# Interleaving the high and the low half of each weight block word by word

## The chip, the cores and the metric

The kernel runs on one core of a Trainium2 chip. The metric is the device time of one execution in microseconds, as the median of several runs. The profile is that of one execution.

## The reference

One step of a decoder layer for 256 prompt rows and 8 sample rows, 264 in all, with shared weights, all in float32:

```
h += 0.5 * swiglu(rmsnorm(h), gate, up, down)      # ffn1: 2048 -> 5504 -> 2048
u  = rmsnorm(h);  z = u @ w_in                     # pooling | RWKV-7 | attention queries | 3 gates
h += (g0 * pool(z) + g1 * rwkv7(z) + g2 * cross_attention(z, memory)) @ w_o
h += 0.5 * swiglu(rmsnorm(h), gate, up, down)      # ffn2
y  = rmsnorm(h)
mem_k, mem_v = rmsnorm(mem) @ w_mem_k, rmsnorm(mem) @ w_mem_v   # 256 memory tokens, 2048 -> 512
```

Outputs are y for both groups, the memory keys and values, and the recurrent states. Nearly all the arithmetic is products of a (264 x 2048) or (264 x 5504) activation with a weight matrix that is read once.

## The kernel before, in words

Activations are kept transposed: a tile holds 128 channels on the partitions and the 264 rows as columns. Each float32 product is made from three matmuls in the type fp32r, which carries fewer bits: every operand is split into a high half (its value rounded to fp32r) and a low half (the rest). The function `mm3` adds hi·hi, hi·lo and lo·hi into one accumulator. In it the weight is the stationary operand, a 128x128 tile that TensorE loads, and the activation is the moving operand, 264 columns.

The weights come as a stream of 783 blocks listed in `specs`, in the order of use. A block is usually eight tiles of 128x128, 1024 words on each partition (512 KB); 747 blocks have that size, 32 have 384 words, 2 have 512 and 2 have 256. `emit_load(i)` issues the transfer of block i on SP's queue into a `raw` buffer (5 of them), has ACT copy it to `whi` in the type fp32r, which rounds, and has DVE subtract `whi` from `raw` into `wlo` (3 buffers of each). `nxt` is called at the use of block i and first emits the loads up to block i + 2, so that a block is split while two earlier ones are multiplied. `proj` runs over the blocks of one output tile and calls `mm3` for each 128x128 tile.

One stage uses the weights differently: `mem_proj` projects the memory tokens. There the split tokens (`m0h`, `m0l`, ...) are the stationary operand, and the weight block is the moving one, 512 columns at a time (L517 to L519; 16 blocks, 192 matmuls).

The stages follow each other: the first feed-forward with the memory projections in its early part, the mixer's input projections with cross-attention and element-wise RWKV work beside them, the gates with the RWKV recurrence in the background (`tri_gen`, `chain_gen`, `sample_gen`, on DVE, POOL and TensorE), the output projections, the second feed-forward, and the last norm. Background work is written as generators, of which `tick` runs the due ones after each block. The instructions of an engine run in the order in which they were issued; the waits between engines are derived from which tiles an instruction reads and writes.

Two lines that the prediction also speaks of are in `tri_gen`, on tiles `c4k` with 32x32 matrices; the second source of the product is a column of the matrix, so its words lie 32 words apart:

```
DVE.tensor_tensor(out=tmp[:, 0:t, 0:t], in0=W[:, 0:t, 0:t],                                   # L977
                  in1=U[:, 0:t, t].unsqueeze(1).broadcast_to([P, t, t]), op=ALU.mult)
DVE.tensor_reduce(out=W[:, 0:t, t], in_=tmp[:, 0:t, 0:t], axis=AX.X, op=ALU.add)              # L979
```

and one is in the attention of the sample rows, where a 128x128 float32 tile is loaded for a moving operand of one column (L788).

Of the kernel before, what the change touches and what calls it, by code (L numbers as in the profile page):

```python
# [9 lines left out]
F32 = mybir.dt.float32  # L10
F32R = mybir.dt.float32r
AF = mybir.ActivationFunctionType
ALU = mybir.AluOpType
AX = mybir.AxisListType

P = 128
# [22 lines left out]
HK = 1024  # L39
# [7 lines left out]
def step_kernel(ctx: ExitStack, tc: tile.TileContext, I, O):  # L47
    nc = tc.nc
    PE, ACT, DVE, POOL, SP = nc.tensor, nc.scalar, nc.vector, nc.gpsimd, nc.sync
    PSUM = bass.MemoryType.PSUM  # L50
    DRAM = bass.MemoryType.DRAM
# [3 lines left out]
    wp = ctx.enter_context(tc.tile_pool(name="wp", bufs=3))  # L55
# [11 lines left out]
    def sb(pool, shape, tag, dt=F32, bufs=None):  # L67
        kw = {} if bufs is None else {"bufs": bufs}
        return pool.tile(shape, dt, tag=tag, name=nm(tag), **kw)

    def ps(shape=(P, 512)):
        return pms.tile(list(shape), F32, tag="ps", name=nm("ps"))
# [4 lines left out]
    def pool_ctx(name, side=None):  # L77
        kw = {} if side is None else {"side": side}
        cm = tc.tile_pool(name=name, bufs=1, reuse_waits="tile", **kw)
        return cm  # L80

# [1 line left out]
    ident = sb(cst, [P, P], "ident")  # L83
    make_identity(nc, ident)
    ones = sb(cst, [P, P], "ones")
# [21 lines left out]
    for t in range(15):  # L107
        DVE.memset(rcnt[:, t:t + 1], 1.0 / (t + 1))

# [1 line left out]
    def flat(a):  # L111
        return a[0]

# [54 lines left out]
    loaded = {}  # L168
# [3 lines left out]
    def emit_load(i):  # L172
        name, w, k0, n, c0, m = specs[i]
        raw = wp.tile([P, HK], F32, tag="raw", name=f"raw{i}", bufs=5)
        rv = raw[:, :n * m].rearrange("p (j c) -> p j c", c=m)
        ws = w if isinstance(w, tuple) else (w,)
        cw = m // len(ws)
        for q, wq in enumerate(ws):
            SP.dma_start(out=rv[:, :, q * cw:(q + 1) * cw],
                         in_=wq[k0 * P:(k0 + n) * P, c0:c0 + cw].rearrange("(j p) c -> p j c", p=P))  # L180
        hi = wp.tile([P, HK], F32R, tag="whi", name=f"whi{i}")
        ACT.activation(hi[:, :n * m], raw[:, :n * m], AF.Copy)  # L182
        lo = wp.tile([P, HK], F32R, tag="wlo", name=f"wlo{i}")
        DVE.tensor_tensor(out=lo[:, :n * m], in0=raw[:, :n * m], in1=hi[:, :n * m].bitcast(F32), op=ALU.subtract)  # L184
        loaded[i] = (hi[:, :n * m].rearrange("p (j c) -> p j c", c=m),
                     lo[:, :n * m].rearrange("p (j c) -> p j c", c=m))

    def spawn(gen, wait=0):
        tasks.append([state["t"] + wait + (not state["in"]), gen])
# [26 lines left out]
    def nxt(name):  # L216
        i = state["i"]
        assert specs[i][0] == name, (specs[i][0], name)
        while state["l"] <= min(i + state["look"], len(specs) - 1):
            emit_load(state["l"])  # L220
            state["l"] += 1
        state["i"] = i + 1
        loaded.pop(i - 3, None)
        tick()
        return loaded[i][0], loaded[i][1], specs[i][3]
# [14 lines left out]
                k += 1  # L240
        return acc

# [1 line left out]
    nstate = {}  # L244

    def norm_begin():
# [51 lines left out]
        later(wait, fin, nstate["sq"])  # L298
        return nstate["xs"], rstd

# [1 line left out]
    def dt_(name, shape):  # L302
        return dr.tile(list(shape), F32, tag=name, name=name)

# [11 lines left out]
    ys_d = dt_("ys_d", [NB, RW])  # L316
    qs_d = dt_("qs_d", [NB, XW])

# [1 line left out]
    hcm = pool_ctx("h1")  # L320
    hp = hcm.__enter__()
    fcm = pool_ctx("f1a")
# [17 lines left out]
    p = ps()  # L340
# [120 lines left out]
            x_squares(c)  # L461
        return accs

# [1 line left out]
    sst = sb(cst, [P, 27, NB], "sst")  # L465
    mx = []

# [69 lines left out]
            DVE.tensor_copy(out=ktt[:, hh:hh + 2, :], in_=p.rearrange("p (q m) -> p q m", q=2))  # L537
        SP.dma_start(out=KT_d, in_=ktt)

# [1 line left out]
    def ffn(pre, h, xs, rstd, done, pool, tpool, first=None, hook=None):  # L541
        gs = [None] * NF

        def glu(f, ag, au):
            t1 = sb(tpool, [P, NT], "t1", bufs=2)
            DVE.tensor_tensor(out=t1, in0=ag[:, :NT], in1=rstd, op=ALU.mult)
            s1 = sb(tpool, [P, NT], "s1", bufs=2)
            ACT.activation(s1, t1, AF.Sigmoid)  # L548
            POOL.tensor_tensor(out=t1, in0=t1, in1=rstd, op=ALU.mult)  # L549
            POOL.tensor_tensor(out=s1, in0=s1, in1=t1, op=ALU.mult)  # L550
            g = sb(tpool, [P, NT], "g", bufs=2)
            DVE.tensor_tensor(out=g, in0=au[:, :NT], in1=s1, op=ALU.mult)  # L552
            gs[f] = split(pool(f), g, f"g{f}")

        for f in range(NF):
            if hook is not None:
                hook(f)
            if f == 0 and first is not None:
                later(3, glu, 0, *first)
                continue  # L560
            ag = proj((pre, "g", f), KD, xs)
            au = proj((pre, "u", f), KD, xs)
            glu(f, ag, au)
        for d in range(KD):
            ad = proj((pre, "d", d), NF, gs)
            DVE.scalar_tensor_tensor(out=h[d], in0=ad[:, :NT], scalar=0.5, in1=h[d], op0=ALU.mult, op1=ALU.add)
            done(d)
# [30 lines left out]
    fcm.__exit__(None, None, None)  # L598
    hcm.__exit__(None, None, None)

# [1 line left out]
    mxcm = pool_ctx("mx")  # L602
    mp = mxcm.__enter__()
    Mcm = pool_ctx("M", side="right")
# [9 lines left out]
    s1cm = pool_ctx("sub1")  # L614
    ew = s1cm.__enter__()

# [1 line left out]
    spr = sb(ew, [120, PW], "BKt")  # L618
    SP.dma_start(out=spr, in_=I["state_pool"][0].rearrange("b r c -> (b r) c"))
    spT = sb(ew, [P, 4, 120], "spT")  # L620
# [17 lines left out]
    for g in range(4):  # L638
# [10 lines left out]
        while sh < w:  # L649
# [3 lines left out]
                               op=ALU.add)  # L653
# [22 lines left out]

    later(4, pool_rows)

# [1 line left out]
    for g in range(4):  # L680
        acc = proj(("zq", g), KD, xs)
        DVE.tensor_tensor(out=qT[g], in0=acc[:, :NT], in1=rstd, op=ALU.mult)
# [113 lines left out]
    spawn(attn_prompt(), 2)  # L796
    spawn(attn_sample(), 2)

# [1 line left out]
    def zmix(acc, m, idx, tag, out=None):  # L800
        z = sb(ew, [P, 15 + NT], "zt", bufs=2)
        POOL.memset(z[:m, 0:1], 0.0)
        DVE.tensor_tensor(out=z[:m, 1:1 + NT], in0=acc[:m, :NT], in1=rstd[:m], op=ALU.mult)
        POOL.tensor_copy(out=zlast[:m, idx, :], in_=z[:m, SEQ:SEQ + 9])
        df = sb(ew, [P, 15 + NT], "diff", bufs=2)
        POOL.tensor_tensor(out=df[:m, 0:SEQ], in0=z[:m, 0:SEQ], in1=z[:m, 1:1 + SEQ], op=ALU.subtract)
        POOL.tensor_tensor(out=df[:m, SEQ:NT], in0=sst[:m, idx, :], in1=z[:m, 1 + SEQ:1 + NT], op=ALU.subtract)
        x = sb(ew, [P, NT], tag) if out is None else out
        DVE.scalar_tensor_tensor(out=x[:m], in0=df[:m, 0:NT], scalar=col("rwkv_mu", idx)[:m],
                                 in1=z[:m, 1:1 + NT], op0=ALU.mult, op1=ALU.add)  # L810
        return x
# [128 lines left out]
        recv_mix(v, ft, acc)  # L940
        later(2, build_m, v, ft)

# [1 line left out]
    rp, s2cm, yT = None, None, None  # L944

    def c4(dt=F32):
# [270 lines left out]
    for dp in range(8):  # L1217
        ms = []
        for b, w, src in ((0, "pool_out", pl), (2, "xattn_out", list(zip(oh, ol)))):
            gt = [gate(b, d) for d in (2 * dp, 2 * dp + 1)]  # L1220
            wh, wl, n = nxt(w)
# [51 lines left out]
    xs, rstd = norm_end()  # L1273
    mhcm.__exit__(None, None, None)

# [1 line left out]
    fcm = pool_ctx("f2")  # L1277
    fp = fcm.__enter__()
    Y = []
# [34 lines left out]
    p = ps()  # L1314
    for i in range(3):
        for q, t in enumerate((sq, sql)):
            PE.matmul(p[:, 2 * i:2 * i + 2], lhsT=sqr[q] if i == 2 else t[:, i * P:(i + 1) * P], rhs=ones[:, 0:2],
                      start=q == 0, stop=q == 1)
# [64 lines left out]
```

## Time and profile before

| | |
|---|---|
| runs, us | 2464.16, 2472.68, 2472.36 (median 2472.36) |
| profiled execution | span 2464.4 us, from first to last instruction; no time of its own beside it is given |
| mean granted TensorE clock | 0.987 of full speed |
| PE matmul busy | 2419.3 us, 19702 matmuls |
| weight loads busy | 2377.5 us, beside the matmuls |
| DVE / ACT / POOL busy | 1452.2 / 1086.5 / 514.6 us |
| memory read | 430.19 MB, 182 GB/s over the span |

Busy times of different engines overlap. [...]

### The profile page before, as it was taken

The page shows a single profiled execution, that of the slowest core. Times are in us where ns is not written, and L with a number is a line of the kernel's source. Part 1 is how long each engine was busy: PE and PEld are TensorE (multiplying, and loading weights), DVE is VectorE, ACT ScalarE, POOL GpSimd, SP SyncE. Part 2 cuts the span into 40 slices and gives each one's busy share as a digit, 9 for nine tenths or more (in the row PEclk, how much of TensorE's full clock was granted, in tenths as well). Part 3 has the DMA queues.
Part 4 walks back from the last instruction along what each step waited for, and adds up shares of the span by engine and source line. Part 5 has one row for each costly group of instructions (what it writes and reads, how often), then busy time and mean ns, then how long its engine had stood idle before and what let it go on. Part 6 is the DMA issues. An engine that isn't in the chain of part 4 may idle for free.

```text
span 2464.4 us, 47553 instructions
## 1 busy us (share of the span) xinstructions
PE 2419.3 (98%) x19702; PEld 2377.5 (96%) x19702; DVE 1452.2 (59%) x1818; ACT 1086.5 (44%) x1436; POOL 514.6 (21%) x593
## 2 busy tenths in 40 slices
PE   8999999999999999999979999999999999999998
PEld 7999999999999988999979999999999999999998
DVE  6655555555444659798894765666555555544444
ACT  6444444444444445454322754444444444444444
POOL 3211211120000225461480210111111211110000
PEclk9999999999999999999889999999999999999999
DMA  8676666666666867676755667776666666666664
GB/s 231 172 216 180 180 179 180 180 180 177 186 189 192 243 181 215 170 185 184 189 157 150 159 181 192 195 220 178 179 180 180 180 180 181 180 173 175 176 182 129
DMA packets 822460, 452.03 MB, mean 183 GB/s; under 512 B 29092, under 2 KB 806982, under 8 KB 821963
## 3 DMA queue, kind: packets, MB, share of 16 engines
q1 hardware_dynamic: 821795, 448.91, 65.2%
q8 instruction: 154, 2.52, 0.4%
q14 instruction: 63, 0.52, 0.1%
q0 software_dynamic: 448, 0.08, 0.0%
HBM read 430.19 MB, written 18.96 MB: 182 GB/s over the span
## 4 chain that ended last, share of the span: by engine, by line
PE 93%; DVE 2%; DMA 2%; issue 1%; POOL 1%; ACT 0%; SPq 0%; DVEq 0%; POOLq 0%; ACTq 0%
PE acc L228 29%; PE acc L230 29%; PE acc L229 28%; DVE wlo L184 1%; DMA qb<-qs_d 1%; POOL kc L746 1%; PE acc L519 1%; PE acc L518 1%; PE acc L517 1%; PE ps L902 1%; PE acc L788 1%; PE ps L1080 0%; PE ps L1056 0%; PE ps L1084 0%; DMA raw<-in_ffn_w_up_dram 0%
## 5 line engine op out<-in xcount | busy, mean ns | idle before, releaser
L184 DVE TENSOR_TENSOR wlo<-raw,whi 128x1024 fp32r<-128x1024 f32 (+2 forms) x783 | 966.1, 1234 | 732.7 <-ACT whi L182 677.2
L182 ACT ACTIVATE whi<-raw 128x1024 fp32r<-128x1024 f32 (+2 forms) x783 | 809.9, 1035 | 1136.3 <-PE acc L229 757.2
L549 POOL TENSOR_TENSOR t<-t,rstd 128x264 f32<-128x264 f32 x86 | 123.0, 1430 | 855.8 <-ACT s L548 843.7
L272 POOL TENSOR_TENSOR sqs<-sqs,sqt 128x264 f32<-128x264 f32 x44 | 41.9, 953 | 547.4 <-ACT sqt L271 547.4
L230 PE MATMUL acc<-x8h,wlo 128*128 128x264 f32 (+1 forms) x255 | 72.9, 286 | 6.8 <-DVE wlo L184 6.8
L230 PE MATMUL acc<-x0h,wlo 128*128 128x264 f32 (+1 forms) x255 | 73.5, 289 | 5.0 <-DVE snm L690 3.6
L228 PE MATMUL acc<-x0h,whi 128*128 128x264 f32 (+1 forms) x255 | 77.8, 305 | 0.0
L228 PE MATMUL acc<-x8h,whi 128*128 128x264 f32 (+1 forms) x255 | 76.8, 302 | 0.0
L228 PE MATMUL acc<-x4h,whi 128*128 128x264 f32 (+1 forms) x255 | 73.5, 289 | 1.3 <-ACT x4h L261 1.3
L552 DVE TENSOR_TENSOR g<-acc,s 128x264 f32<-128x264 f32 x86 | 37.2, 432 | 63.4 <-PE acc L230 61.2
L230 PE MATMUL acc<-x1h,wlo 128*128 128x264 f32 (+1 forms) x255 | 73.9, 290 | 0.0
L229 PE MATMUL acc<-x1l,whi 128*128 128x264 f32 (+1 forms) x255 | 73.8, 290 | 0.0
L230 PE MATMUL acc<-x13h,wlo 128*128 128x264 f32 (+1 forms) x255 | 73.8, 289 | 0.0
L230 PE MATMUL acc<-x2h,wlo 128*128 128x264 f32 (+1 forms) x255 | 73.6, 289 | 0.0
L230 PE MATMUL acc<-x9h,wlo 128*128 128x264 f32 (+1 forms) x255 | 73.6, 289 | 0.0
L230 PE MATMUL acc<-x5h,wlo 128*128 128x264 f32 (+1 forms) x255 | 73.6, 289 | 0.0
L229 PE MATMUL acc<-x9l,whi 128*128 128x264 f32 (+1 forms) x255 | 73.6, 289 | 0.0
L228 PE MATMUL acc<-x12h,whi 128*128 128x264 f32 (+1 forms) x255 | 73.5, 288 | 0.0
L228 PE MATMUL acc<-x2h,whi 128*128 128x264 f32 (+1 forms) x255 | 73.5, 289 | 0.0
L229 PE MATMUL acc<-x2l,whi 128*128 128x264 f32 (+1 forms) x255 | 73.5, 288 | 0.0
L228 PE MATMUL acc<-x11h,whi 128*128 128x264 f32 (+1 forms) x255 | 73.4, 289 | 0.0
L229 PE MATMUL acc<-x13l,whi 128*128 128x264 f32 (+1 forms) x255 | 73.4, 288 | 0.0
(1168 smaller groups left out, 8893.7 us busy)
## 6 DMA issues: line engine op xcount, KB each, us to landing
raw<-in_ffn_w_gate_dram SPq DMA_DIRECT2D x170, 512.0 KB
raw<-in_ffn_w_up_dram SPq DMA_DIRECT2D x170, 512.0 KB
raw<-in_w_in_dram SPq DMA_DIRECT2D x164, 512.0 KB
raw<-in_ffn_w_down_dram SPq DMA_DIRECT2D x160, 512.0 KB
raw<-in_w_o_dram SPq DMA_DIRECT2D x32, 512.0 KB
raw<-in_rwkv_out_dram SPq DMA_DIRECT2D x16, 512.0 KB
raw<-in_ffn_w_down_dram SPq DMA_DIRECT2D x32, 192.0 KB
raw<-in_w_mem_k_dram SPq DMA_DIRECT2D x8, 512.0 KB
```

What stands on the lines that cost most here:

```text
L182: ACT.activation(hi[:, :n * m], raw[:, :n * m], AF.Copy)
L184: DVE.tensor_tensor(out=lo[:, :n * m], in0=raw[:, :n * m], in1=hi[:, :n * m].bitcast(F32), op=ALU.subtract)
L228: PE.matmul(out, lhsT=wh, rhs=xh, start=first, stop=False)
L229: PE.matmul(out, lhsT=wh, rhs=xl, start=False, stop=False)
L230: PE.matmul(out, lhsT=wl, rhs=xh, start=False, stop=last)
L272: POOL.tensor_tensor(out=sq, in0=sq, in1=t, op=ALU.add)
L517: PE.matmul(accs[i], lhsT=xh, rhs=wh[:, j, :], start=k == 0, stop=False)
L518: PE.matmul(accs[i], lhsT=xh, rhs=wl[:, j, :], start=False, stop=False)
L519: PE.matmul(accs[i], lhsT=xl, rhs=wh[:, j, :], start=False, stop=k == 15)
L549: POOL.tensor_tensor(out=t1, in0=t1, in1=rstd, op=ALU.mult)
L552: DVE.tensor_tensor(out=g, in0=au[:, :NT], in1=s1, op=ALU.mult)
L746: POOL.tensor_tensor(out=kcs[b], in0=kcs[b], in1=qbs[b].unsqueeze(1).broadcast_to([P, 2, XW]), op=ALU.mult)
```

## The change

The two buffers `whi` and `wlo` become one, `whl`, with two words for each weight: the high half at even words and the low half at odd words. ACT writes the high halves with a step of 8 bytes, DVE reads them with that step and writes the low halves with it, and TensorE reads either half with it, as stationary operand in `mm3` and as moving operand in `mem_proj`. There are three buffers as before, of twice the size. Five comment lines elsewhere are removed.

```
-        hi = wp.tile([P, HK], F32R, tag="whi", name=f"whi{i}")
-        ACT.activation(hi[:, :n * m], raw[:, :n * m], AF.Copy)
-        lo = wp.tile([P, HK], F32R, tag="wlo", name=f"wlo{i}")
-        DVE.tensor_tensor(out=lo[:, :n * m], in0=raw[:, :n * m], in1=hi[:, :n * m].bitcast(F32), op=ALU.subtract)
-        loaded[i] = (hi[:, :n * m].rearrange("p (j c) -> p j c", c=m),
-                     lo[:, :n * m].rearrange("p (j c) -> p j c", c=m))
+        hl = wp.tile([P, HK, 2], F32R, tag="whl", name=f"whl{i}")
+        hi, lo = hl[:, :n * m, 0], hl[:, :n * m, 1]
+        ACT.activation(hi, raw[:, :n * m], AF.Copy)
+        DVE.tensor_tensor(out=lo, in0=raw[:, :n * m], in1=hi.bitcast(F32), op=ALU.subtract)
+        loaded[i] = (hi.rearrange("p (j c) -> p j c", c=m), lo.rearrange("p (j c) -> p j c", c=m))
```

## Rows read from the trace of the kernel before

**Rows 1.** The page's first part: busy time, share of the span, instructions.
```profile
PE 2419.3 (98%) x19702; PEld 2377.5 (96%) x19702; DVE 1452.2 (59%) x1818; ACT 1086.5 (44%) x1436; POOL 514.6 (21%) x593
```

**Rows 2.** Busy time of each engine by stage; the stage is from:to and its length.
```profile
core 0: us, PE busy (x) PEld busy (x) DVE busy (x) ACT busy (x) POOL busy (x), PEclk, DMA share, GB/s
400.00:800.00 400.00, 400.00 (x3283) 400.00 (x3283) 201.78 (x218) 167.80 (x203) 43.92 (x44) 1.00 0.65 184
...
1150.00:1290.00 140.00, 122.68 (x1195) 119.00 (x1194) 124.28 (x108) 42.24 (x54) 76.24 (x38) 0.90 0.63 175
800.00:1150.00 350.00, 342.76 (x2705) 330.58 (x2704) 268.64 (x419) 172.77 (x240) 141.82 (x255) 0.98 0.73 198
```

**Rows 3.** The chain that ended last, share of the span by line.
```profile
by line: PE acc L228 28.6%; PE acc L230 28.6%; PE acc L229 28.2%; DVE wlo L184 1.1%; issue 1.1%; DMA qb<-qs_d 0.9%; POOL kc L746 0.8%; PE acc L518 0.6%; PE acc L519 0.6%; PE acc L517 0.6%; PE ps L902 0.6%; PE acc L788 0.5%; PE ps L1080 0.4%
```

**Rows 4.** Timeline in the first feed-forward: start, duration (us), engine, line.
```profile
400.67 0.28 PE L228 MATMUL acc<-x9h,whi 128*128 128x264 f32 x1
400.67 0.19 PEld L229 LDWEIGHTS acc<-x9l,whi 128*128 128x128 f32 x1
400.79 0.29 PE L229 MATMUL acc<-x9l,whi 128*128 128x264 f32 x1
400.79 0.19 PEld L230 LDWEIGHTS acc<-x9h,wlo 128*128 128x128 f32 x1
400.92 0.29 PE L230 MATMUL acc<-x9h,wlo 128*128 128x264 f32 x1
```

**Rows 5.** Timeline at the end of the memory projections.
```profile
143.73 0.40 PE L517 MATMUL acc<-whi,m15h 128*128 128x512 f32 x1
143.96 0.40 PE L518 MATMUL acc<-wlo,m15h 128*128 128x512 f32 x1
...
144.89 0.40 PE L519 MATMUL acc<-whi,m15l 128*128 128x512 f32 x1
145.13 0.28 PE L228 MATMUL acc<-x0h,whi 128*128 128x264 f32 x1
```

**Rows 6.** The chain in order of time around 977: one-column matmuls.
```profile
977.48 1.68 PE acc L788 x16
```

**Rows 7.** Who waited for whom on TensorE and its loads: us, times, longest.
```profile
PEld acc L230 <- DVE wlo L184: 14.4, 8, 3.8
...
PE acc L230 <- DVE wlo L184: 9.1, 5, 3.4
```

**Rows 8.** DVE and ACT by line and form: count | busy us, mean ns | idle before.
```profile
L184 DVE TENSOR_TENSOR wlo<-raw,whi 128x1024 fp32r<-128x1024 f32 x747 | 946.0, 1267 | 695.5 <-ACT whi L182 640.0 <-PE acc L229 52.7 <-PE acc L230 1.7
...
L977 DVE TENSOR_TENSOR c4k<-c4k,c4k 128x961 f32<-128x961 f32 x1 | 2.0, 2000 | 0.0
...
L979 DVE TENSOR_REDUCE c4k<-c4k 128x31 f32<-128x961 f32 x1 | 1.2, 1159 | 0.0
...
L977 DVE TENSOR_TENSOR c4k<-c4k,c4k 128x400 f32<-128x400 f32 x1 | 0.9, 904 | 0.0
...
L184 DVE TENSOR_TENSOR wlo<-raw,whi 128x256 fp32r<-128x256 f32 x2 | 0.8, 420 | 0.3 <-ACT whi L182 0.3
...
L979 DVE TENSOR_REDUCE c4k<-c4k 128x20 f32<-128x400 f32 x1 | 0.6, 572 | 0.0
...
L182 ACT ACTIVATE whi<-raw 128x384 fp32r<-128x384 f32 x32 | 16.8, 526 | 58.1 <-PE acc L229 58.1
```

**Rows 9.** The two lines of the split: duration ns min/median/max.
```profile
L184 DVE TENSOR_TENSOR wlo<-raw,whi x783: 415/1226/4697, 7.6 to 2444.3; 128x1024 fp32r<-128x1024 f32 x179, 128x384 fp32r<-128x384 f32 x16, 128x512 fp32r<-128x512 f32 x1
...
L182 ACT ACTIVATE whi<-raw x783: 416/1060/1066, 6.4 to 2443.8; 128x1024 fp32r<-128x1024 f32 x179, 128x384 fp32r<-128x384 f32 x16, 128x512 fp32r<-128x512 f32 x1
```

**Rows 10.** Busy time of L184 alone in the two mixer stages.
```profile
1150.00:1290.00 140.00, 50.78 (x31) 0.90 0.63 175
800.00:1150.00 350.00, 118.16 (x95) 0.98 0.73 198
```

## The prediction

> **What bounds the kernel now.** I read the page's first part, then the busy time by stage, then the chain of waits, and last single rows of the timeline. The page shows TensorE busy for nearly the whole span, and its weight loads almost as much, because a load runs beside the matmul before it [rows 1]. [...] The exceptions are the mixer's recurrence (1150 to 1290), where DVE has 124.3 of 140 us, and the stage before it (800 to 1150) [rows 2]. The chain that ended last is 85% the three matmul lines of `mm3`; DVE's `wlo` has 1.1% of it, some 27 us [rows 3]. So a change to the weight blocks is worth what it does to the time of one matmul, unless it makes `whi` and `wlo` late.
>
> What sets the time of a matmul? From 400 to 800 there are 3283 in 400.0 us, 121.8 ns each, all with 264 moving columns. The timeline shows the load of the next weights starting with each matmul and the next matmul 0.12 us later [rows 4]; that alone does not say which of the two paces the pair. The memory projections do: they load the same 128x128 stationary tiles but move 512 columns, and start every 0.23 us, six of them in 1.40 us (143.73 to 145.13), so 233.3 ns each [rows 5]. The difference, 111.5 ns for 248 columns, is 0.450 ns a column, and 264 x 0.450 = 118.7 leaves 3 ns fixed. The moving stream paces the pair; the load is hidden. How well it is hidden is seen where the moving operand is one column wide: 16 such pairs take 1.68 us, 105 ns each or 0.82 ns a weight column [rows 6]. So a load has 121.8 - 105 = 16.8 ns of cover: it may grow to 0.95 ns a column for nothing, and beyond that every ns is paid by each `mm3` matmul. Counted from the specs there are 17,904 of these, and 192 matmuls in the memory projections.
>
> **What is changed.** No instruction is added, removed or reordered in the source: 783 loads of 512 KB or less, 783 ACT copies, 783 DVE subtractions, the same matmuls, and the same three buffers' worth of bytes. SP's and POOL's queues get the same issues. What changes is the step of four accesses and the waits on the shared buffer.
>
> *Waits.* One buffer now holds both halves. ACT's write of a block must wait for the last matmul on `lo` (L230) of the block three earlier, not the last on `hi` (L229): 0.12 us later. Behind it in ACT's queue stand sigmoids and splits, but a block is due only after two more blocks, 2 x 24 x 121.8 ns = 5.85 us, and the work is 1.06 + 1.23 us, so this costs nothing outside the recurrence. And if the waits follow the span of addresses, not the single words, the first matmul of a block (L228) waits for DVE's `lo`, which today only the third does. Today that wait shows 8 times at the load and 5 times at the matmul [rows 7]. Each would begin two matmuls earlier: 13 x 2 x 121.8 ns = 3.2 us. Bounds 0 and 3.2; I take 3.2.
>
> *The steps.* No row shows a step of 8 bytes, so I bound it. Contiguous slopes: DVE 1.05 ns a word ((1226 - 420) / 768), ACT 0.83 ((1060 - 526) / 640, with the 526 a mean) [rows 8, 9]; the weight load 0.82; the moving operand 0.450. The other end is L977, a DVE product whose second source steps 128 bytes a word: from 400 to 961 words it grows by 1096 ns, 1.95 ns a word, while the reduction L979 over as many contiguous words grows by 587 ns, 1.05 [rows 8]. So a step can cost, and 1.95 ns a word is the worst that a row shows. What lies between? [...] If memory fetches whole stretches and a step of 8 bytes uses half of them, a stepped word cannot come faster than 2 x 0.450 = 0.90 ns. This is an estimate from these rows, and it is the nearer of the two ends (two words are 8 bytes apart, not 128). It gives:
> - weight loads: 128 x 0.90 = 115 ns, under 121.8: hidden, 0 us. Ends: 0, and 128 x 1.95 = 250 ns, which is 128 ns on each of 17,904, 2290 us.
> - memory projections, the only place where the weights are the moving operand: 512 x 0.90 = 461 + 3 ns, +231 ns on each of 192, 44.3 us, all on PE's chain, which has no gap there [rows 5]. Nothing gives it back: the stages behind are PE's too. Ends: 0, and 512 x (1.95 - 0.45) = 768 ns, 147 us.
> - DVE: 0.90 is under its 1.05: nothing. Upper end: one 1.95 covers reading and writing with a step, +0.92 us a block.
> - ACT: 0.83 to 0.90, +0.07 us a block, hidden. Upper end 1.95: +1.15 us a block, hidden too (ACT's 1087 us and 783 x 1.15 make 1987 of 2464).
>
> Sum: 3.2 + 44.3 = 47.5 us. It stands against the profiled execution: span 2464.4, close to the lowest run shown, 2464.16, so nearly nothing lies around it. That makes 2511.9. The median of the three runs, 2472.36, is 8.0 above that span; the forecast, given as a median, is 2519.9, say 2520.
>
> [...] L977 shows that single words far apart cost DVE 1.95 ns instead of 1.05 [rows 8]. [...]
>
> **The rivals.**
> *A. All steps are free.* Then only the waits are left: 2464.4 + 3.2 + 8.0 = 2476, no measurable change. For it: DVE, ACT and the loads each take a word at under half the moving stream's rate, so half-used fetches are enough for them. Against: the memory projections take words at the full rate. It decides if their matmuls stay at 233 ns. [...] 0.29.
> *B. The weight load becomes the bound.* Its place is every `mm3`; it decides above 0.95 ns a weight column, and each 0.1 ns more is 12.8 ns x 17,904 = 229 us. At 1.05 (DVE's rate) +0.10: some 230 + 47, about 2750; at 1.95, about 4800. For it: the cover is only 16.8 ns, 16%, and the load is the largest user of the new step. Against: at 0.90 it fits, and a load needs a word only every 0.82 ns. A small excess (0.97) is +46 us, about 2565. [...] 0.20, of which a quarter stays under 2600.
> *C. DVE and ACT pay, the load doesn't.* In the feed-forwards it is hidden: 783 x 0.92 on 1452 us of DVE is still 88% of the span. In the recurrence 31 subtractions gain 28.5 us where DVE has 15.7 us idle; from 800 to 1150 there are 95, 87 us where it has 81 [rows 2, 10]. With late `wlo` on top, +20 to +70 us; with the moving operand's 44, about 2565. Where they are hidden, the cover is the 5.85 us ahead against 2.2 + 2.15. 0.07.
> *D. Faster.* No work is taken away; only another order from the scheduling or fewer waits in the recurrence could give it. 0.03, about 2455.
>
> **How the numbers follow.** My forecast (loads hidden, the projections at half rate) has 0.41, from 2500 to 2545. A has 0.29, B 0.20, C 0.07, D 0.03. A measurement here tells about 0.5%, 12 us, from no change. Faster 0.03 (D); same 0.29 (A, and forecasts in which the projections lose less than 10 us); slower 0.68 (forecast, B, C). The range must hold A and C and the small excess of B: 2463 to 2595. Left out are the large part of B, 0.15, and most of D.
>
> **What the profile after would show.** Right: L517 to L519 start every 0.46 us and the stage from 99 to 145 is some 44 us longer; L228 to L230 still start every 0.122 us; the one-column rows unchanged; the 1024-word subtraction still near 1.23 us, the copy 1.06 to 1.13; waits on `wlo` named at L228. Wrong: projections at 0.23 us (A); a pace of `mm3` over 0.125 us all along (B); a subtraction of 2 us (C). [...]

## The result and the profile after

The changed kernel takes 2533.16 us as the median of three runs (2532.57 to 2537.61), against 2472.36 before: a ratio of 1.0266, 95% interval 1.0249 to 1.0282. The profiled execution grew from 2464.4 to 2531.4 us, by 67.0. The lines of the code have moved up by one: `mm3` is L227 to L229, the memory projections are L516 to L518, the copy is L183, and the subtraction is still L184.

The page of the changed kernel, first part:

```profile
PE 2488.1 (98%) x19702; PEld 2407.1 (95%) x19702; DVE 1446.2 (57%) x1818; ACT 1147.8 (45%) x1436; POOL 527.9 (21%) x593
```

TensorE is busy for the same 98% as in [rows 1], with the same 19702 matmuls, and takes 69 us longer over them. Nothing began to starve it (it is idle for 43.3 us, before for 45.1); its own instructions became slower. Where they did is read from the timeline of the memory projections (start, duration) and, for `mm3`, from the busy time by stage, first of the changed kernel and then of the kernel before. In each of the last three windows both kernels are in the same stage:

```profile
145.30 0.65 PE L516 MATMUL acc<-whl,m15h 128*128 128x512 f32 x1
145.75 0.65 PE L517 MATMUL acc<-whl,m15h 128*128 128x512 f32 x1
146.21 0.65 PE L518 MATMUL acc<-whl,m15l 128*128 128x512 f32 x1
...
149.38 0.65 PE L518 MATMUL acc<-whl,m0l 128*128 128x512 f32 x1
```
```profile
core 0: us, PE busy (x) PEld busy (x) DVE busy (x) ACT busy (x) POOL busy (x), PEclk, DMA share, GB/s
400.00:800.00 400.00, 400.00 (x3234) 400.00 (x3233) 201.39 (x221) 175.10 (x201) 56.70 (x49) 1.00 0.64 180
...
210.00:330.00 120.00, 120.00 (x976) 120.00 (x975) 61.59 (x71) 53.07 (x62) 22.59 (x20) 1.00 0.63 177
640.00:820.00 180.00, 180.00 (x1450) 180.00 (x1449) 86.41 (x89) 78.18 (x90) 12.79 (x10) 1.00 0.65 185
2270.00:2430.00 160.00, 160.00 (x1301) 160.00 (x1301) 71.09 (x80) 73.15 (x89) 15.41 (x9) 1.00 0.63 177
```
```profile
210.00:330.00 120.00, 120.00 (x984) 120.00 (x983) 62.63 (x72) 49.77 (x62) 23.86 (x21) 1.00 0.64 180
640.00:820.00 180.00, 180.00 (x1482) 180.00 (x1482) 91.68 (x94) 77.36 (x93) 9.16 (x14) 1.00 0.66 187
2270.00:2430.00 160.00, 160.00 (x1315) 160.00 (x1315) 75.82 (x80) 70.46 (x90) 10.86 (x10) 1.00 0.63 178
```

From 145.30 to 149.38 there are nine steps from one start to the next, 0.453 us each, where [rows 5] have 0.233. The records are longer than the steps, 0.65 and 0.40 us, so that neighbours overlap; a matmul is counted here by the step. 220 ns on each of 192 matmuls is 42.2 us. The second view is the more surprising one: 3234 matmuls in 400 us instead of 3283 [rows 2], 123.7 ns each instead of 121.8, at the same clock of 1.00. The loss differs by stage: 1.0 ns in the first gate and up stage (976 matmuls instead of 984 from 210 to 330), 2.7 in the first down stage (1450 instead of 1482 from 640 to 820), 1.3 in the second down stage (1301 instead of 1315 from 2270 to 2430). A matmul that only reaches into a window is counted with it, so the differences are surer than the levels. Some 1.4 ns on each of 17,904 is 25 us, and 42 and 25 make the 67 us.

The two engines of the split, by line (duration ns min/median/max), and the waits on the low half (us, times, longest):

```profile
L184 DVE TENSOR_TENSOR whl<-raw,whl x783: 417/1227/8460, 7.5 to 2511.7; 128x1024 fp32r<-128x1024 f32 x179, 128x384 fp32r<-128x384 f32 x16, 128x512 fp32r<-128x512 f32 x1
...
L183 ACT ACTIVATE whl<-raw x783: 434/1152/1216, 6.3 to 2511.1; 128x1024 fp32r<-128x1024 f32 x179, 128x384 fp32r<-128x384 f32 x16, 128x512 fp32r<-128x512 f32 x1
```
```profile
PEld acc L229 <- DVE whl L184: 20.0, 6, 7.0
...
PE acc L229 <- DVE whl L184: 15.5, 5, 6.8
```

The subtraction, which reads and writes with the step, has the median that it had (1227 ns, 1226 in [rows 9]); the copy went from 1060 to 1152 ns, 0.09 us. The wait for the low half still stands at the third matmul, not the first: the waits tell interleaved words apart. It is some 6 us longer in all than in [rows 7], but TensorE's idle time as a whole is not.

### The profile page after: what moved, and what is told of

Its sections match the earlier page's. It is cut to its first block, busy times and chain, and to the rows that moved or that the text cites. A ratio compares the mean times of both kernels' runs of the same rounds, so it can differ in the third digit from the quotient of the medians.

```text
span 2531.4 us, 47454 instructions
## 1 busy us (share of the span) xinstructions
PE 2488.1 (98%) x19702; PEld 2407.1 (95%) x19702; DVE 1446.2 (57%) x1818; ACT 1147.8 (45%) x1436; POOL 527.9 (21%) x593
## 4 chain that ended last, share of the span: by engine, by line
PE 90%; DVE 5%; issue 2%; DMA 1%; SPq 0%; ACT 0%; POOL 0%; DVEq 0%; POOLq 0%; ACTq 0%
PE acc L229 27%; PE acc L227 27%; PE acc L228 27%; DVE whl L184 2%; PE acc L518 1%; PE acc L516 1%; PE acc L517 1%; DVE c4k L976 1%; PE ps L901 1%; PE acc L787 1%; DVE c4k L978 0%; PE ps L1079 0%; DMA qb<-qs_d 0%; PE ps L1042 0%; POOL kc L745 0%
## 5 line engine op out<-in xcount | busy, mean ns | idle before, releaser
L184 DVE TENSOR_TENSOR whl<-raw,whl 128x1024 fp32r<-128x1024 f32 (+2 forms) x783 | 975.1, 1247 | 798.0 <-ACT whl L183 797.3
L183 ACT ACTIVATE whl<-raw 128x1024 fp32r<-128x1024 f32 (+2 forms) x783 | 878.9, 1124 | 1172.0 <-PE acc L229 746.5
L229 PE MATMUL acc<-x0h,whl 128*128 128x264 f32 (+1 forms) x255 | 74.6, 293 | 13.3 <-DVE whl L184 9.9
L227 PE MATMUL acc<-x0h,whl 128*128 128x264 f32 (+1 forms) x255 | 78.3, 307 | 0.0
L229 PE MATMUL acc<-x8h,whl 128*128 128x264 f32 (+1 forms) x255 | 74.5, 292 | 3.9 <-DVE whl L184 3.9
L227 PE MATMUL acc<-x8h,whl 128*128 128x264 f32 (+1 forms) x255 | 77.2, 304 | 0.0
L229 PE MATMUL acc<-x4h,whl 128*128 128x264 f32 (+1 forms) x255 | 75.3, 295 | 0.0
L229 PE MATMUL acc<-x2h,whl 128*128 128x264 f32 (+1 forms) x255 | 75.3, 295 | 0.0
L229 PE MATMUL acc<-x3h,whl 128*128 128x264 f32 (+1 forms) x255 | 74.8, 293 | 0.0
L229 PE MATMUL acc<-x12h,whl 128*128 128x264 f32 (+1 forms) x255 | 74.8, 293 | 0.0
L228 PE MATMUL acc<-x4l,whl 128*128 128x264 f32 (+1 forms) x255 | 74.4, 292 | 0.2 <-DVE x4l L261 0.2
L228 PE MATMUL acc<-x2l,whl 128*128 128x264 f32 (+1 forms) x255 | 74.4, 292 | 0.0
L229 PE MATMUL acc<-x1h,whl 128*128 128x264 f32 (+1 forms) x255 | 74.4, 292 | 0.0
L227 PE MATMUL acc<-x4h,whl 128*128 128x264 f32 (+1 forms) x255 | 73.5, 289 | 0.9 <-ACT x4h L260 0.9
L227 PE MATMUL acc<-x6h,whl 128*128 128x264 f32 (+1 forms) x255 | 74.2, 292 | 0.0
L227 PE MATMUL acc<-x2h,whl 128*128 128x264 f32 (+1 forms) x255 | 74.1, 292 | 0.0
L229 PE MATMUL acc<-x5h,whl 128*128 128x264 f32 (+1 forms) x255 | 74.0, 290 | 0.0
L229 PE MATMUL acc<-x10h,whl 128*128 128x264 f32 (+1 forms) x255 | 74.0, 290 | 0.0
```

The source lines that it names most:

```text
L183: ACT.activation(hi, raw[:, :n * m], AF.Copy)
L184: DVE.tensor_tensor(out=lo, in0=raw[:, :n * m], in1=hi.bitcast(F32), op=ALU.subtract)
L227: PE.matmul(out, lhsT=wh, rhs=xh, start=first, stop=False)
L228: PE.matmul(out, lhsT=wh, rhs=xl, start=False, stop=False)
L229: PE.matmul(out, lhsT=wl, rhs=xh, start=False, stop=last)
```

## The experiments

Of the twelve kernels nine start from the changed one; narrow_before, cols216_before and tokens_step start from the kernel before. The first five ran in several rounds beside the kernel before; the others ran once, and of them the starts in the trace count, not the time.

**Which blocks cost what.** In two kernels only some of the blocks are interleaved, and the others lie in two contiguous parts of the same shared buffer.

```
         hl = wp.tile([P, HK, 2], F32R, tag="whl", name=f"whl{i}")
-        hi, lo = hl[:, :n * m, 0], hl[:, :n * m, 1]
+        fl = hl.rearrange("p a b -> p (a b)")
+        hi, lo = ((fl[:, :n * m], fl[:, n * m:2 * n * m]) if str(name).startswith("w_mem")
+                  else (hl[:, :n * m, 0], hl[:, :n * m, 1]))       # mem_halves; in mem_only the other way round
```

mem_halves: 

> The changed kernel, but the 16 blocks of the memory projections keep their high halves in the first and their low halves in the second part of the shared buffer. Theory 1 (the step slows the moving stream, 220 ns on each of 192 matmuls): 42 us less than the changed kernel, about 2491, with L516 to L518 back at 0.233 us and L227 to L229 still at 0.1233. Rival (the extra time comes from the shared buffer's waits): no more than a few us less.

mem_only: 

> The reverse: only the blocks of the memory projections are interleaved, all others lie in two parts of the shared buffer. Theory 1: 42 us over the kernel before, about 2510 to 2515; L227 to L229 at 0.1218 us; in the projections the loads of contiguous weights are again longer (0.208 us instead of 0.188), since only the moving operand has the step. Rival (waits): 2535.

Measured: 2492.47 us for mem_halves (ratio 1.0087, 1.006 to 1.0115) and 2510.5 for mem_only (1.0169, 1.0148 to 1.0189), against 2469.62 for the kernel before, measured beside them. So the projections' blocks are worth 41.7 us (36.6 to 46.7) and all the others 21.5 us (14.8 to 28.4). Together that is 63 us, where the medians differ by 61 and the spans by 67. Of the projections in the trace of mem_only, the matmuls and loads with `m0l`, the low halves of the tokens' first 128 channels (ns min/median/max), and then the same of the kernel before. The loaded operand, the tokens, is contiguous in both:

```profile
L519 PE MATMUL acc<-whl,m0l x4: 649/649/649, 102.6 to 147.5; 128*128 128x512 f32 x4
...
L519 PEld LDWEIGHTS acc<-whl,m0l x4: 207/207/208, 102.2 to 147.0; 128*128 128x128 f32 x4
```
```profile
L519 PEld LDWEIGHTS acc<-whi,m0l x4: 188/188/188, 99.7 to 122.8; 128*128 128x128 f32 x4
L519 PE MATMUL acc<-whi,m0l x4: 392/394/395, 99.9 to 123.0; 128*128 128x512 f32 x4
```

The matmul is recorded with 649 instead of 394 ns, and the load with 207 instead of 188, although it has no step itself. That costs nothing here, with 453 ns from start to start.

**Whose step it is.** The shared buffer without any step; the step at TensorE alone; the step at ACT and DVE alone. In the last two TensorE reads the other layout than was written, so that it multiplies other words, and the sizes and instructions stay.

```
-        hi, lo = hl[:, :n * m, 0], hl[:, :n * m, 1]
+        fl = hl.rearrange("p a b -> p (a b)")
+        hi, lo = fl[:, :n * m], fl[:, n * m:2 * n * m]      # halves and pe_steps; split_steps keeps the line above
         ACT.activation(hi, raw[:, :n * m], AF.Copy)
         DVE.tensor_tensor(out=lo, in0=raw[:, :n * m], in1=hi.bitcast(F32), op=ALU.subtract)
+        hi, lo = hl[:, :n * m, 0], hl[:, :n * m, 1]         # pe_steps; split_steps: the two parts; halves: none
```

halves: 

> One shared buffer, high halves in its first part, low halves in its second, no step anywhere. It leaves the waits of the shared buffer alone. Theory 1: 0 to 4 us over the kernel before (2472 to 2476), L228 to L230 (here L227 to L229) at 0.1218 us. Rival (waits or order make the 1.5 ns a matmul, or a good part of the 61 us): 2480 or more.

pe_steps: 

> ACT and DVE write two contiguous parts; TensorE alone reads with the step of 8 bytes, and so multiplies other words than it should; the instructions and sizes are the same. Theory 1 (all of the cost is TensorE's reading): as the changed kernel, 2525 to 2537, the copy back at 1.06 us. Rival (the stepped writes of ACT and DVE slow TensorE's reads, 1.5 ns a matmul): 2508, with L227 to L229 at 0.1218 us.

split_steps: 

> ACT and DVE write and read with the step, TensorE reads two contiguous parts, which hold other words than it should multiply; the instructions and sizes are the same. Theory 1: as before, 2465 to 2478, with the copy at 1.15 us hidden. Rival (stepped writes slow TensorE): 1.5 ns x 17904 = 27 us more, about 2499.

Measured: halves 2466.74 us (ratio 0.9985, 0.9971 to 0.9998), pe_steps 2532.4 (1.0258, 1.0237 to 1.0279), split_steps 2473.07 (1.0005, 0.9991 to 1.0019). The stage from 400 to 800 of halves, pe_steps and split_steps, in this order:

```profile
400.00:800.00 400.00, 400.00 (x3283) 400.00 (x3282) 202.22 (x219) 165.18 (x204) 52.45 (x44) 1.00 0.65 184
```
```profile
400.00:800.00 400.00, 400.00 (x3234) 400.00 (x3233) 200.28 (x220) 162.80 (x201) 55.50 (x48) 1.00 0.64 181
```
```profile
400.00:800.00 400.00, 400.00 (x3284) 400.00 (x3283) 201.96 (x218) 174.73 (x204) 51.79 (x44) 1.00 0.65 184
```

The count of matmuls goes with TensorE's reading alone: 3234 where it steps, 3283 and 3284 where it doesn't, whoever else steps. The shared buffer and its waits cost nothing that can be measured, though TensorE and its loads wait for the low half in halves at least as long as in the changed kernel (19.7 and 21.7 us); the stepped copy and subtraction cost nothing either, since they are hidden. All of the 61 us is TensorE's.

**A step of 16 bytes.** The steps are doubled to 16 bytes where the buffer has room. The 8.9 bytes per ns that the expectation speaks of are one word of 4 bytes in the 0.450 ns a column that the prediction reads from [rows 5].

```
+        if n * m in (384, 512):
+            h4 = hl.rearrange("p (a f) b -> p a (f b)", f=2)
+            hi, lo = h4[:, :n * m, 0], h4[:, :n * m, 1]
```

step16: 

> The changed kernel with a step of 16 bytes in the blocks of 384 and 512 words; the memory projections' blocks are cut to 512 words (32 instead of 16 blocks) so that all of them have it. If memory delivers at 8.9 bytes per ns whatever of them is used: 1.80 ns a word, so the 512-column matmuls start every 0.92 us (192 x 0.47 = 90 us over the changed kernel) and the matmuls of the 384-word blocks, with a load of 230 ns, every 0.23 us (288 x 0.107 = 31 us): about 2650. If the stretch that memory fetches is 8 bytes: 0.453 and 0.123 us as with 8 bytes, about 2535. One look, so the starts in the timeline decide.

One execution took 2573 us, near neither forecast, and the trace says why: the moving operand followed one theory and the load the other. First the projections, then the last tiles of a down projection (384-word blocks), and ACT and DVE by form:

```profile
130.12 0.66 PE L521 MATMUL acc<-whl,m9h 128*128 128x512 f32 x1
...
133.81 0.66 PE L520 MATMUL acc<-whl,m11h 128*128 128x512 f32 x1
...
714.06 0.40 PE L231 MATMUL acc<-g40h,whl 128*128 128x264 f32 x1
714.29 0.40 PE L232 MATMUL acc<-g40l,whl 128*128 128x264 f32 x1
714.53 0.40 PE L233 MATMUL acc<-g40h,whl 128*128 128x264 f32 x1
...
715.94 0.40 PE L233 MATMUL acc<-g42h,whl 128*128 128x264 f32 x1
```
```profile
L187 ACT ACTIVATE whl<-raw 128x512 fp32r<-128x512 f32 x34 | 39.3, 1157 | 50.5 <-PE acc L522 43.8 <-issue 5.8 <-DMA raw<-in_ffn_w_up_dram 0.9
L187 ACT ACTIVATE whl<-raw 128x384 fp32r<-128x384 f32 x32 | 28.9, 904 | 58.4 <-PE acc L233 58.4
...
L188 DVE TENSOR_TENSOR whl<-raw,whl 128x512 fp32r<-128x512 f32 x34 | 38.4, 1128 | 49.7 <-ACT whl L187 49.6
L188 DVE TENSOR_TENSOR whl<-raw,whl 128x384 fp32r<-128x384 f32 x32 | 28.0, 874 | 48.1 <-ACT whl L187 48.1
```

The moving operand takes eight steps from 130.12 to 133.81, 0.461 us each, 0.90 ns a column: as much as with 8 bytes (0.88), and in both about twice the contiguous 0.45. A load takes 235 ns (714.06 to 715.94, eight), 1.84 ns a word, and `mm3` runs at the load's pace there: 288 matmuls x 0.11 us, 32 of the 40 us. ACT and DVE go up to 1.98 ns a word (253 and 254 ns for 128 words). With 8 bytes ACT took 0.93 ns a word ((1152 - 556) / 640, from the changed kernel) and DVE 1.05 ((1227 - 417) / 768), and the load takes 0.93 by cols216_step below. So for these three the step from 8 to 16 bytes makes a word 1.9 to 2.1 times as long.

**How long a load is.** First one matmul in three was cut to 8 columns, in the changed kernel and in the kernel before; then all matmuls but those of the first tile of each sum to 216 columns, in both. What is cut is left out of the sums.

```
-        PE.matmul(out, lhsT=wh, rhs=xl, start=False, stop=False)
+        PE.matmul(out[:, 0:8], lhsT=wh, rhs=xl[:, 0:8], start=False, stop=False)      # narrow_*
...
+        c = NT if first else 216                                                      # cols216_*
+        PE.matmul(out[:, :c], lhsT=wh, rhs=xh[:, :c], start=first, stop=False)        # and so the other two
```

narrow_step: 

> The changed kernel; the second matmul of each three moves 8 columns instead of 264, so that the rest of the high-by-low product is left out. After it the next load is in the open: the distance from L228 to L229 is a load of stepped weights. Theory 1 (0.90 ns a word): 115 ns, 10 more than in the same kernel without the step. If the load is as fast as a contiguous one and the 1.5 ns have another source: 105 as there.

narrow_before: 

> The kernel before with the same 8-column second matmul (the rest of the high-by-low product left out): the distance from L229 to L230 is a load of contiguous weights, 105 ns as where one column moves (L788). If the load of fp32r weights is not paced like that of float32 ones: another number, to which the stepped one is compared.

cols216_before: 

> The kernel before with all matmuls of mm3 but the first of each accumulation moving 216 columns (48 columns of the activations are left out of most of each sum). Moving would take 216 x 0.45 + 3 = 100 ns; so the pace is that of the contiguous load: 113.5 ns if the one 8-column matmul showed it rightly, 8 ns under the 121.8 of 264 columns; 105 if the float32 rows hold.

cols216_step: 

> The same 216 columns in the changed kernel: the pace is that of a load with the step of 8 bytes. If a word takes half of the 1.84 ns that one word in 16 bytes takes: 117.6 ns, 4 ns over the contiguous one and still under 121.8. If the stepped load is really as long as the 123 to 124 ns of the changed kernel's mm3: 123 ns here too, and the load is the bound there.

The totals of the narrow pair (2573.57 and 2494.83) can't be compared, since TensorE's granted clock was 0.62 from 5 to 60 us and 0.50 from 60 to 100 in narrow_step, and 1.00 in narrow_before; the stages at clock 1.00 can. For narrow_before and narrow_step, one stage each:

```profile
400.00:500.00 100.00, 100.00 (x840) 100.00 (x839) 52.99 (x62) 42.43 (x52) 19.85 (x18) 1.00 0.66 184
```
```profile
400.00:500.00 100.00, 100.00 (x825) 100.00 (x823) 52.55 (x61) 44.24 (x51) 19.96 (x18) 1.00 0.65 182
```

Three matmuls take 357.1 ns; less two of 121.95 leaves 113 for the one whose load is in the open. With the step 363.6 less two of 122.95 leaves 118. The contiguous load was expected at 105 ns, as [rows 6] had been read; the next section shows what is wrong in that reading. The stages of cols216_before and cols216_step say the same more directly:

```profile
210.00:330.00 120.00, 120.00 (x1071) 120.00 (x1070) 68.16 (x79) 53.85 (x67) 24.60 (x22) 1.00 0.70 197
```
```profile
210.00:330.00 120.00, 120.00 (x1012) 120.00 (x1010) 64.05 (x73) 54.53 (x64) 23.82 (x21) 1.00 0.66 185
```

112.0 ns a matmul without the step and 118.6 with it: 0.875 and 0.93 ns a weight word. The step costs a load 5 to 7 ns, and the stepped load is still shorter than the 121.9 of the moving stream.

**Why does it cost anything, if it fits?** Two kernels: stepped loads under 512 contiguous columns (the kernel before with the memory tokens interleaved), and stepped loads of only 96 columns under 264.

```
+            ml = sb(st, [P, NM, 2], f"m{j}", F32R)                                          # tokens_step
+            split_into(ml[:, :, 0], ml[:, :, 1], p[:, :NM], col("mem_norm_g", j))
...
+        q = wh.shape[-1] if first or last else min(96, wh.shape[-1])                        # load96
+        PE.matmul(out[:q], lhsT=wh[:, :q], rhs=xh, start=first, stop=False)                 # and so the other two
```

tokens_step: 

> The kernel before; only the split memory tokens are interleaved with a step of 8 bytes. They are the stationary operand of the memory projections, so that here loads with a step run under 512 contiguous moving columns, with over 100 ns of cover. If a stepped load costs only by what sticks out of the matmul before it: L517 to L519 start every 0.2333 us as before. If it takes reads from the moving stream (the theory for the 1 to 2.7 ns that mm3 lost): 1 to 3 ns more each, 0.234 to 0.236 us, and the recorded load at 0.198 us or more instead of 0.188. The total is unchanged either way (0.5 us at most).

load96: 

> The changed kernel, but all matmuls of mm3 except the first and the last three of each accumulation load only 96 of the 128 weight columns (32 output channels are left out of most of each sum), so that the stepped load takes about 0.925 x 96 = 89 ns and ends long before the 264 moving columns. If mm3 lost its 1 to 2.7 ns because a load of 118 ns ends too near to the 122 ns of the moving stream: L227 to L229 (here three lines of mm3) start every 0.1219 us or less. If each stepped load takes reads from the moving stream: three quarters of the loss stay, 0.1227 us in the first feed-forward's gate and up stage. The first and last tiles of each accumulation keep 128 columns, which is 2 of 16 tiles there, and add at most 0.15 ns to the mean.

tokens_step: the timeline of the projections, and the recorded loads (ns min/median/max):

```profile
120.29 0.39 PE L520 MATMUL acc<-wlo,m 128*128 128x512 f32 x1
...
121.91 0.40 PE L519 MATMUL acc<-whi,m 128*128 128x512 f32 x1
```
```profile
L519 PEld LDWEIGHTS acc<-whi,m x64: 193/195/199, 105.8 to 150.4; 128*128 128x128 f32 x64
```

Seven starts from 120.29 to 121.91, 0.231 us each (0.232 over the 55 from 106.12 to 118.89), where it was 0.233: the recorded load is 7 ns longer (195 instead of 188), and the moving stream has lost nothing. So here, where a load of 118.6 ns lies under 231, it does not disturb the matmul above it. load96, the first gate and up stage and the first down stage:

```profile
210.00:330.00 120.00, 120.00 (x981) 120.00 (x980) 61.69 (x72) 52.90 (x61) 23.99 (x22) 1.00 0.63 179
640.00:820.00 180.00, 180.00 (x1471) 180.00 (x1470) 90.05 (x93) 80.62 (x93) 14.40 (x11) 1.00 0.66 186
```

122.3 ns in the first, between the 121.95 of before and the 122.95 of the changed kernel, and 122.4 in the second, between 121.5 and 124.1. The tiles that kept 128 columns account for 0.1 of it. So in the others, where the load ends some 30 ns earlier (32 words at 0.93), some 70% of the loss is gone in both stages. A loss by loaded words would have shrunk by a quarter, one that only a late end makes would have gone.

Nor is the loss even within a tile. By the starts in the traces, from 210 to 330 the distances behind the first, second and third matmul of a tile grow by 0.3, 0.3 and 2.8 ns, and from 640 to 820 by 0.9, 6.3 and 1.1, while in cols216_step the load is no longer in the second stage than in the first: 118.1 ns (508 matmuls in the 60 us from 620 to 680) and 118.6.

## Why the prediction was right

- *TensorE's pace is what counts, nothing else.* Right, and shown by halves, pe_steps and split_steps: the buffer, its waits and the work of ACT and DVE move nothing.
- *Memory projections at half rate, +231 ns on 192 matmuls, 44.3 us.* Right in place and size: 220 ns, 42.2 us in the trace, 41.7 by mem_only. The reason given was half right. The 0.90 ns for a stepped word was the author's estimate, twice the contiguous 0.450, and no run shows that memory fetches whole stretches at a fixed rate. As a number it fits what the runs show of all four accesses at 8 bytes: 0.88 for the moving operand, 0.93 for the load, 0.93 for ACT (1152 ns for 1024 words, 556 for 384), and DVE's 1.05, which lies above it. But it is not a byte rate that every step must pay for: at 16 bytes the moving operand pays no more (0.90), and the others do (1.84 to 1.98). Why they differ is not shown.
- *Weight loads hidden, 0 us.* This is the term that was mis-sized: it measured 21.5 us (14.8 to 28.4). The estimate for the stepped load, 115 ns, was near the 118.6 measured, and the verdict that it is shorter than the matmul was right. What failed is the overlap: a load that fits under the moving stream was taken for free, and one that ends 3 ns before it loses 1.0 to 2.7 ns a matmul. The cover was misread too, as the lines below this list show: 10 ns, not 16.8, and the step takes 6.6 of them. This alone would have left the term at 0, since 118.6 still fits.
- *Why it loses them* is only partly settled. That a stepped load disturbs whatever stream runs above it is excluded by tokens_step. That the loss comes from the load ending too near to the matmul's own end fits load96 for the larger part; the rest stays open, and so does why the loss is 1.0 ns in one stage and 2.7 in another, and sits at one of three matmuls, with the same instructions and other addresses.
- *ACT 0.07 us a block, DVE nothing, both hidden.* Right: 0.09 us and 0.
- *Waits, 0 to 3.2 us.* The lower bound held, 0 of the 3.2 that were taken: the wait stayed at the third matmul, and halves is at 0.9985 of the kernel before.
- *The sum.* 47.5 us were forecast, and the span grew by 67.0: 25 more by the loads, 2 less by the projections, 3 less by the waits. The median grew by 60.8 only, because the 8.0 us between span and median came out as 1.8. That the forecast is only 13 us too low owes 6 us to this, and that is luck.
- *The rivals.* A, all steps free, fell with the projections. What spoke for it, that DVE, ACT and the loads take words at under half the moving stream's rate, held for DVE alone: half of that rate is a word in 0.90 ns, and ACT took one in 0.83, the load in 0.875. Free at 8 bytes was DVE alone (1227 ns, before 1226); ACT paid 9% (1152 and 1060 ns) and the load 6% (118.6 and 112.0), and at 16 bytes all three paid: 1.98, 1.98 and 1.84 ns a word. C named DVE and ACT as those that pay. DVE, which reads one source and writes with the step, paid 1 ns of 1226, and ACT's 92 ns stayed hidden. B came true in small: not a load that is the bound, but one without room.

The misread cover: [rows 6] were divided into sixteen distances of 105 ns. But that row begins at 977.48, when the first of the sixteen matmuls, started at 977.32, is all but over, so it holds fifteen distances of 112 ns. The timeline of TensorE before, and what these matmuls are recorded with (ns min/median/max):

```profile
977.32 1.84 PE L788 MATMUL acc<-prT,kc 128*128 128x1 f32 x16
...
977.45 1.70 PE L788 MATMUL acc<-prT,kc 128*128 128x1 f32 x14
...
L788 PE MATMUL acc<-prT,kc x128: 165/250/250, 971.6 to 1014.2; 128*128 128x1 f32 x128
```

The second row leaves the first two of the sixteen out. Less the 0.25 us that the last is recorded with, it is 13 distances in 1.45 us, 112 ns each, as in cols216_before.

No version beats the kernel before: two contiguous parts in a shared buffer (halves) are as fast, within what a measurement tells.

## What to carry to other kernels

Before a layout with a step is chosen, measure which engine reads it at which rate: here 8 bytes were free for DVE (1226 to 1227 ns), 9% for ACT (1060 to 1152), 6% for a weight load (112.0 to 118.6), and half the rate for the moving operand of an fp32r matmul (233 to 453). Here weight load and matmul ran side by side at 112 and 122 ns, and a load grown by 6.6 ns already cost 1.0 to 2.7 ns a matmul: on 17,904 instructions that was 0.9% of the time (21.5 us). Measure such a load in its own stream, and count distances, not instructions, in a merged row: sixteen matmuls taken for sixteen distances made the load 7 ns too short.

## What was not expected

- A load of 128 columns cost 112 ns, in fp32r under 216 moving columns (cols216_before) as in float32 beside one (L788 of the kernel before), and the step of 8 bytes added 6.6 (cols216_step).
- The moving operand took 0.45 ns a word when contiguous [rows 5], 0.88 with 8 bytes (the changed kernel) and 0.90 with 16 (step16); the load took 0.875, 0.93 and 1.84 (cols216_before, cols216_step, step16).
- The moving operand with the step came with a recorded load of 207 instead of 188 ns beside it, though the loaded operand was contiguous (mem_only).
